# Last down projection and final norm in segments of 384 and 128 tokens instead of 256 and 256

## The chip, the cores and the metric

The kernel runs on one core of a Trainium2 chip. The time is the device time of one execution in microseconds; the time before is the median of 3 runs, 1311.32 us (1310.68 to 1312.76). A core has five engines that run side by side, each with its own instruction list worked off in order: TensorE (PE, matrix products; PEld is its weight load), VectorE (DVE), ScalarE (ACT), GpSimd (POOL) and SyncE (SP, which only issues transfers). They wait for each other through semaphores.

## The reference, cut to what matters

One layer: a half-step SwiGLU FFN on 512 latent and 256 context tokens, a mixer, then for the 512 latent tokens a second half-step FFN and the final RMSNorm. Only the end is touched:

```python
def rmsnorm(x, w):
    xf = x.astype(jnp.float32)
    y = xf * lax.rsqrt(jnp.mean(xf * xf, axis=-1, keepdims=True) + EPS)
    return (y * w.astype(jnp.float32)).astype(x.dtype)

def swiglu(h, w1, w2):
    g, u = jnp.split(h @ w1, 2, axis=-1)
    return (jax.nn.silu(g) * u) @ w2

x = x + 0.5 * gate * swiglu(modulate(rmsnorm(x, norm3_w), shift, scale), w1, w2)   # x: 512 x 1024, w2: 2816 x 1024
return rmsnorm(x, final_norm_w)
```

## The kernel before, in words

Features lie on the partitions and tokens on the free axis: the stream `x` is 8 tiles (m = 0 to 7) of 128 features by 512 tokens, float32. Each float32 product is made as three products of rounded parts (`gemm3`: high by high, high by low, low by high), all of type float32r, which TensorE takes as one instruction, where plain float32 leaves two records in the trace.

The second FFN (`ffn2`) makes 22 hidden tiles of 128 features. Their down projection is done two hidden tiles at a time, 512 tokens wide, while the up projection goes on (`turns`, banks named `aux`). The last two hidden tiles are kept for the end (`last`), and `down_last` does them in two segments of tokens, one after the other; call them A and B. In a segment `down` makes for each m six products (2 hidden tiles by 3) into one bank named `mm` (there are five), then:

- VectorE evicts: `x = bank * gate + x` (`stt`, called the eviction below);
- ScalarE squares x (`sq_add`) into `rms_acc` (the first of a lane) or `nm_t` (the later ones, of which so many buffers are there as `bufs` says), and then scales x in place by the weight of the final norm;
- VectorE (lane v) or GpSimd (lane p) adds `nm_t` to the accumulator of its lane. The last m have lanes of their own, with nothing to add.

When a segment's eight m are out, `after` queues its norm: TensorE sums each accumulator over the partitions by products with a column of ones (`rms_sum`, plain float32, one per accumulator and 128 tokens), VectorE adds the epsilon (`hms`), GpSimd takes the power -1/2 (`hr`), VectorE spreads it over a diagonal (`dg`), TensorE turns this into one row for all partitions (`rms_spread`), VectorE multiplies x by it, two m at a time (`then` in `build`, tile `s`, called the scaling below), and SP sends each pair of m to the output. Behind segment B eight products that nobody reads (`busy` in `after`) run while its norm is waited for.

What sets the order: a scheduler places every engine's instructions when the kernel is built, from the order in which the code calls them and what they depend on. So A's norm is laced into B's products, and the places are fixed before the kernel runs. `sq_add` also serves the end of the first FFN (three segments of 256 tokens) and the end of the mixer, with the same buffer names.

Of the kernel before, what the change touches and what calls it, by code (L numbers as in the profile page):

```python
# [7 lines left out]
F32 = mybir.dt.float32  # L8
# [4 lines left out]
P = 128  # L13
DM = 1024
KT = DM // P
NC_ = 256
# [10 lines left out]
CTX, LAT, LAT_A, LAT_B = (0, NC_), (NC_, NL), (NC_, 256), (NC_ + 256, 256)  # L27
# [42 lines left out]
class Space1:  # L70
# [16 lines left out]
    gate = lambda self, j: self.rows(j, 1)  # L87
# [11 lines left out]
class Builder:  # L99
# [13 lines left out]
    def sq_add(self, S, k, x, n, lanes="vpvpvpvl"):  # L113

        nc = self.nc
        lane = lanes[k]
        if n > 512:
            sq = self.tmp.tile([P, n], F32)
        elif lane in S:
            sq = self.tmp.tile([P, n], F32, name="nm_t", bufs=3)  # L120
        else:
            sq = self.tmp.tile([P, n], F32, name="rms_acc", bufs=6)
        nc.scalar.activation(sq, x, AF.Square)
        if lane not in S:
            S[lane] = sq
            return lambda: None
        eng = nc.gpsimd if lane == "p" else nc.vector
        return lambda: eng.tensor_tensor(out=S[lane], in0=S[lane], in1=sq, op=ALU.add)
# [434 lines left out]
    def ffn2(self, w1, w2, gate, first, then, final, fast):  # L563
        nc = self.nc
        G = 2

        def load2(j):
            w2r = self.fp.tile([P, DM], F32, name="w2raw", bufs=2)
            w2h = self.fp.tile([P, DM], F32R, name="w2hi", bufs=3)
            w2l = self.fp.tile([P, DM], F32R, name="w2lo", bufs=3)  # L570
            nc.sync.dma_start(out=w2r, in_=w2[j])
            return w2h, w2l, w2r

        def mm(part, half, k):
            ws, pss = part
            h, l = (w[:, k * P:(k + 1) * P] for w in ws[half])
            self.gemm3(pss[half], h, l, self.xh[k][:, NC_:], self.xl[k][:, NC_:], k, KT)

        class Space:
            sums = lambda _, j: (fast["s"][:, 2 * (j % 2) + i, :] for i in range(2))  # L580
            last = lambda _: [self.fp.tile([P, DM // 2], F32R, name="wd" + x, bufs=2) for x in "hl"]
            up = lambda _, j: self.fp.tile([P, 2, 256], F32, name="ev", bufs=2)
            gate = lambda _, j: self.fp.tile([P, NL], F32, name="sg", bufs=2)
        space = Space()

        def act_tiles():
            return [self.fp.tile([P, NL], F32R, name=n, bufs=3) for n in ("ah", "al")]

        def gated(part, sg, lo, n):

            g, u = (p[:, lo - NC_:lo - NC_ + n] for p in part[1])
            sg = sg[:, lo - NC_:lo - NC_ + n]
            nc.scalar.activation(sg, g, AF.Silu)
            self.tt(sg, u, sg, ALU.mult)

        def act(part, j):
            w2, sg, (ah, al) = load2(j), space.gate(j), act_tiles()
            gated(part, sg, *LAT)
            self.split(ah, al, sg)
            self.split(*w2)  # L600
            return w2[0], w2[1], ah, al

        def up(j):
            part = self.ffn_load(w1, j)
            for half in range(2):
                for k in range(KT):
                    mm(part, half, k)
            return act(part, j)

        parts, turns, late = [], [], {}  # L610

        def done(part):
            parts.append(part)
            if len(parts) == G:
                both = parts[:]
                parts.clear()
                turns.extend(lambda m=m: self.down(both, LAT, m, 1, self.aux, gate, off=NC_) for m in range(KT))

        def turns_take(n=NT):
            for _ in range(min(n, len(turns))):  # L620
                turns.pop(0)()

        def turn(j, at):
            if at == 3:
                late[j] = load2(j)
                self.split(*late[j])
            if j < NJ - 1 or at in (0, 2, 4):
                turns_take(1)

        def gated_fast(j, sg):  # L630
            ah, al = act_tiles()
            self.split(ah, al, sg)
            done((late[j][0], late[j][1], ah, al))
        for j, part in enumerate(first):
            done(act(part, j))
        for j in range(2, fast["first"]):
            if j == fast["first"] - 1:
                fast["s"] = fast["make"]()
            part = up(j)
            turns_take()  # L640
            done(part)
        unit = lambda j: self.up_half(w1, j, 256, NC_, fast["t"], space, j == NJ - 1)
        nxt = unit(fast["first"])
        next(nxt), next(nxt)
        last = []

        def end(j, sg):

            if j < NJ - 1:
                return gated_fast(j, sg)  # L650
            ah, al = act_tiles()
            for c in (0, 256):
                self.split(*(t[:, c:c + 256] for t in (ah, al, sg)))
            last.extend((*parts, (late[j][0], late[j][1], ah, al)))
        self.ups_half(range(fast["first"], NJ), unit, nxt, turn, end)
        turns_take()
        self.down_last(last, [(seg, gate) for seg in (LAT_A, LAT_B)], then, final=final, off=NC_)

    def fast_operands(self, pool, first=4):

# [914 lines left out]
```

## Time and profile before

| | |
|---|---|
| median of 3 runs | 1311.32 us |
| profiled execution, its own time | 1312.59 us |
| its span in the trace | 1310.8 us |
| PE busy | 1286.0 us (98%) |
| DVE, ACT, POOL busy | 1012.4, 578.0, 56.5 us |
| last product of segment B ends | 1297.56 us |
| last scaling of the norm ends | 1306.78 us |

The span is what the profiler saw from the first to the last instruction; the execution's own time lies 1.79 us above it. PE is busy nearly all the time, so for most of the kernel a change counts only as far as it moves PE. In the last 13 us PE has no more large products, and the time is set by the chain of the norm.

### The profile page before, as it was taken

The page shows a single profiled execution, that of the slowest core. Times are in us where ns is not written, and L with a number is a line of the kernel's source. Part 1 is how long each engine was busy: PE and PEld are TensorE (multiplying, and loading weights), DVE is VectorE, ACT ScalarE, POOL GpSimd, SP SyncE. Part 2 cuts the span into 40 slices and gives each one's busy share as a digit, 9 for nine tenths or more (in the row PEclk, how much of TensorE's full clock was granted, in tenths as well). Part 3 has the DMA queues.
Part 4 walks back from the last instruction along what each step waited for, and adds up shares of the span by engine and source line. Part 5 has one row for each costly group of instructions (what it writes and reads, how often), then busy time and mean ns, then how long its engine had stood idle before and what let it go on. Part 6 is the DMA issues. An engine that isn't in the chain of part 4 may idle for free.

```text
span 1310.8 us, 20560 instructions
## 1 busy us (share of the span) xinstructions
PE 1286.0 (98%) x8210; PEld 1179.8 (90%) x8210; DVE 1012.4 (77%) x1620; ACT 578.0 (44%) x992; POOL 56.5 (4%) x81
## 2 busy tenths in 40 slices
PE   8999999999999999999989999999999999999997
PEld 4689999999998888999978798889998999999996
DVE  6995778777789888767676867986588788888766
ACT  5553444444442222383457343444473444444434
POOL 2000000000000000110100000000000000000001
PEclk8999999999999999999989999999999999999998
DMA  9224443344686866413041101114233222233301
GB/s 347 106 93 151 140 146 125 133 140 145 214 289 228 271 209 195 145 47 117 3 145 49 65 34 49 65 50 175 83 107 136 97 97 97 102 108 104 106 17 65
DMA packets 48803, 163.60 MB, mean 125 GB/s; under 512 B 5554, under 2 KB 10034, under 8 KB 48708
## 3 DMA queue, kind: packets, MB, share of 16 engines
q1 hardware_dynamic: 46308, 150.50, 33.4%
q0 software_dynamic: 2400, 11.80, 2.8%
q8 instruction: 64, 1.05, 0.3%
q14 instruction: 31, 0.25, 0.1%
HBM read 149.39 MB, written 12.89 MB: 124 GB/s over the span
## 4 chain that ended last, share of the span: by engine, by line
PE 94%; DVE 2%; ACT 2%; issue 1%; POOL 0%; DMA 0%; POOLq 0%; DVEq 0%
PE mm L56 72%; PE aux L56 21%; DVE mod_scr L56 1%; ACT xh L56 1%; DVE x L56 0%; ACT nm_y L56 0%; ACT x L56 0%; DVE wlo L56 0%; ACT nm_t L56 0%; ACT whi L56 0%; DVE xl L56 0%; POOL rms_acc L56 0%; DVE s L56 0%; DVE nm_x L56 0%; DMA four<-in_cc 0%
## 5 line engine op out<-in xcount | busy, mean ns | idle before, releaser
L56 PE MATMUL mm<-xh,whi 128*128 128x256 f32 (+2 forms) x1072 | 345.7, 323 | 1.2 <-ACT xh L56 1.2
L56 PE MATMUL mm<-xh,wlo 128*128 128x256 f32 (+2 forms) x1072 | 342.4, 320 | 0.8 <-DVE wlo L56 0.8
L56 PE MATMUL mm<-xl,whi 128*128 128x256 f32 (+2 forms) x1000 | 323.4, 324 | 2.9 <-DVE xl L56 2.9
L56 PEld LDWEIGHTS mm<-xh,whi 128*128 128x128 f32 x1072 | 203.3, 190 | 14.3 <-ACT xh L56 1.9
L56 PEld LDWEIGHTS mm<-xh,wlo 128*128 128x128 f32 x1072 | 203.4, 190 | 10.8 <-DVE wlo L56 1.0
L56 PE MATMUL mm<-six,whi 128*128 128x384 f32 (+1 forms) x752 | 209.3, 359 | 0.0
L56 PEld LDWEIGHTS mm<-xl,whi 128*128 128x128 f32 x1000 | 189.8, 190 | 14.7 <-DVE xl L56 4.3
L56 ACT ACTIVATE whi<-wraw 128x1024 fp32r<-128x1024 f32 x100 | 105.9, 1062 | 170.4 <-PE aux L56 91.5
L56 PEld LDWEIGHTS mm<-six,whi 128*128 128x128 f32 x752 | 135.7, 188 | 10.0
L56 PE MATMUL mm<-six,wlo 128*128 128x384 f32 (+1 forms) x376 | 134.4, 357 | 0.0
L56 DVE TENSOR_TENSOR wlo<-wraw,whi 128x1024 fp32r<-128x1024 f32 x100 | 121.7, 1219 | 10.5 <-ACT whi L56 10.4
L56 DVE CUSTOM_DVE_ANT_0 mod_scr<-wm,cb 128x1024 bf16<-128x1024 f32 x84 | 105.4, 1255 | 2.8 <-DMA wm<-in_w_mod 2.6
L56 PEld LDWEIGHTS mm<-six,wlo 128*128 128x128 f32 x376 | 70.6, 188 | 6.5
L56 DVE SCALAR_TENSOR_TENSOR x<-mm,mod_l,x 128x256 f32<-128x256 f32 (+1 forms) x88 | 51.9, 601 | 18.3 <-PE mm L56 17.5
L56 DVE TENSOR_TENSOR wlo<-four,whi 128x1024 fp32r<-128x1024 f32 x37 | 45.3, 1225 | 26.7 <-ACT whi L56 26.7
L56 PE MATMUL aux<-ah,w2hi 128*128 128x512 f32 x160 | 64.0, 400 | 0.0
L56 ACT ACTIVATE whi<-four 128x1024 fp32r<-128x1024 f32 x37 | 39.2, 1061 | 56.1 <-PE mm L56 46.1
L56 PE MATMUL aux<-al,w2hi 128*128 128x512 f32 x160 | 63.1, 394 | 0.0
L56 DVE SCALAR_TENSOR_TENSOR x<-aux,mod_l,x 128x512 f32<-128x512 f32 x80 | 58.9, 745 | 5.2 <-PE aux L56 5.2
L56 PE MATMUL aux<-ah,w2lo 128*128 128x512 f32 x160 | 62.4, 390 | 0.0
L56 PE MATMUL mm<-tl,whi 128*128 128x256 f32 x216 | 61.0, 283 | 0.0
L56 PE MATMUL aux<-six,whi 128*128 128x256 f32 x320 | 59.0, 282 | 0.0
(336 smaller groups left out, 2553.8 us busy)
## 6 DMA issues: line engine op xcount, KB each, us to landing
wraw<-in_f1w SPq DMA_DIRECT2D x62, 512.0 KB, 3.9
wm<-in_w_mod SPq DMA_DIRECT2D x58, 512.0 KB, 4.0
wraw<-in_f2w SPq DMA_DIRECT2D x44, 512.0 KB, 3.4
wraw<-in_wi SPq DMA_DIRECT2D x32, 512.0 KB, 3.3
w2raw<-in_f2w SPq DMA_DIRECT2D x22, 512.0 KB, 4.2
four<-h SPq DMA_DIRECT2D x22, 384.0 KB, 4.7
h<-x POOLq DMA_DIRECT2D x18, 384.0 KB, 3.0
wraw<-in_wo SPq DMA_DIRECT2D x8, 512.0 KB, 4.0
```

Source lines behind the costliest of these rows:

```text
L56: r = f(*a, **kw)
```

## The change

Segments A and B of `down_last` in `ffn2` are 384 and 128 tokens instead of 256 and 256. To fit in memory, `nm_t` has 2 buffers instead of 3 and `rms_acc` 3 instead of 6, everywhere that `sq_add` is called; squares of 128 tokens get a name of their own with 4 buffers.

```diff
         elif lane in S:
-            sq = self.tmp.tile([P, n], F32, name="nm_t", bufs=3)
+            sq = self.tmp.tile([P, n], F32, name="nm_t", bufs=2)
+        elif n == P:
+            sq = self.tmp.tile([P, n], F32, name="rms_last", bufs=4)
         else:
-            sq = self.tmp.tile([P, n], F32, name="rms_acc", bufs=6)
+            sq = self.tmp.tile([P, n], F32, name="rms_acc", bufs=3)
...
-        self.down_last(last, [(seg, gate) for seg in (LAT_A, LAT_B)], then, final=final, off=NC_)
+        self.down_last(last, [((NC_, 384), gate), ((NC_ + 384, P), gate)], then, final=final, off=NC_)
```

The order moves in two places. First VectorE at the end, from the first scaling of segment A on (`s` is the scaled output, `x<-mm` an eviction of B, `hms` the start of B's norm). Before:

```order
L56 TENSOR_TENSOR s<-x,aux 128x2x256
L56 SCALAR_TENSOR_TENSOR x<-mm,mod_l,x 128x256
L56 TENSOR_TENSOR rms_acc<-rms_acc,nm_t 128x256
L56 TENSOR_TENSOR s<-x,aux 128x2x256
L56 SCALAR_TENSOR_TENSOR x<-mm,mod_l,x 128x256
L56 TENSOR_TENSOR s<-x,aux 128x2x256 x2
L56 TENSOR_SCALAR hms<-aux 128x2
```

The same stretch now, with the last three evictions of B between the scalings:

```order
L56 TENSOR_TENSOR s<-x,aux 128x2x384
L56 TENSOR_TENSOR rms_last<-rms_last,nm_t 128x128
L56 TENSOR_TENSOR s<-x,aux 128x2x384
L56 SCALAR_TENSOR_TENSOR x<-mm,mod_l,x 128x128
L56 TENSOR_TENSOR s<-x,aux 128x2x384
L56 SCALAR_TENSOR_TENSOR x<-mm,mod_l,x 128x128
L56 TENSOR_TENSOR s<-x,aux 128x2x384
L56 SCALAR_TENSOR_TENSOR x<-mm,mod_l,x 128x128
L56 TENSOR_SCALAR hms<-aux 128x1
```

Before, two scalings stood ahead of the last eviction and two behind it; now all four, each half as wide again, stand ahead of it, and three evictions stand behind the first scaling instead of two.

The second place is TensorE at the start of the mixer's projections, where the norm of the first FFN's last segment is summed (`rms_acc` 5029, 5047, 5128 are its three accumulators). Here the sums stand in the difference as taken out:

```order
 L56 MATMUL mm_5138<-xh_86,whi_4801 128x256
-L56 MATMUL aux_5201<-ones_80,rms_acc_5029 128x1 x2
-L56 MATMUL aux_5201<-ones_80,rms_acc_5047 128x1 x2
-L56 MATMUL aux_5201<-ones_80,rms_acc_5128 128x1 x2
 L56 MATMUL mm_5138<-xl_87,whi_4801 128x256
```

And here as put in, six products later:

```order
 L56 MATMUL mm_5138<-xh_86,whi_4801 128x256
+L56 MATMUL aux_5201<-ones_80,rms_acc_5029 128x1 x2
+L56 MATMUL aux_5201<-ones_80,rms_acc_5047 128x1 x2
+L56 MATMUL aux_5201<-ones_80,rms_acc_5128 128x1 x2
 L56 MATMUL mm_5138<-xl_87,whi_4801 128x256
```

The sums of that segment moved behind six products of 256 columns.

## Rows read from the trace of the kernel before

**Rows 1.** The page's chain that ended last: shares of the span by engine.
```profile
PE 94%; DVE 2%; ACT 2%; issue 1%; POOL 0%; DMA 0%; POOLq 0%; DVEq 0%
```
**Rows 2.** Stretches: us, busy by engine (instructions), granted clock (1.00 is full), DMA, GB/s.
```profile
1283.45:1297.56 14.11, 13.96 (x111) 13.34 (x109) 11.74 (x27) 10.89 (x30) 3.47 (x5) 1.00 0.01 2
1297.56:1306.78 9.22, 4.40 (x26) 3.62 (x26) 5.91 (x12) 2.14 (x5) 1.08 (x2) 0.67 0.41 145
1306.78:1310.80 4.02, 0.00 (x0) 0.00 (x0) 0.00 (x0) 0.00 (x0) 0.00 (x0) 0.50 0.55 189
```
**Rows 3.** Timeline of PE at the end: start, us, instruction, count [idle before it].
```profile
1292.33 1.05 PE L56 MATMUL aux<-ones,rms_acc 128*128 128x1 f32 x8
...
1297.28 0.28 PE L56 MATMUL mm<-ah,w2lo 128*128 128x256 f32 x1
1298.27 0.61 PE L56 MATMUL aux<-ones,rms_acc 128*128 128x1 f32 x4 [0.71 <-DVE rms_acc L56]
...
1300.66 0.82 PE L56 MATMUL aux<-ones,rms_acc 128*128 128x1 f32 x4
1303.07 1.19 PE L56 MATMUL aux<-dg,ones 128*128 128x256 f32 x2 [1.59 <-DVE dg L56]
```
**Rows 4.** Timeline of DVE at the end.
```profile
1286.46 2.05 DVE L56 SCALAR_TENSOR_TENSOR x<-mm,mod_l,x 128x256 f32<-128x256 f32 x5 [0.26 <-PE mm L56]
...
1297.53 0.68 DVE L56 TENSOR_TENSOR rms_acc<-rms_acc,nm_t 128x256 f32<-128x256 f32 x1
...
1298.74 0.47 DVE L56 SCALAR_TENSOR_TENSOR x<-mm,mod_l,x 128x256 f32<-128x256 f32 x1
...
1302.49 0.42 DVE L56 TENSOR_TENSOR dg<-ident,hr 128x256 f32<-128x256 f32 x1 [0.82 <-POOL hr L56]
1304.30 2.48 DVE L56 TENSOR_TENSOR s<-x,aux 128x512 f32<-128x512 f32 x4 [1.38 <-PE aux L56]
```
**Rows 5.** Timeline of ACT at the end.
```profile
1290.67 0.71 ACT L56 ACTIVATE nm_t<-x 128x256 f32<-128x256 f32 x2
...
1292.09 0.71 ACT L56 ACTIVATE rms_acc<-x 128x256 f32<-128x256 f32 x2
...
1299.24 0.42 ACT L56 ACTIVATE rms_acc<-x 128x256 f32<-128x256 f32 x1 [0.38 <-DVE x L56]
```
**Rows 6.** Chain, merged: products of 384 columns, then of 256 (start, us, count).
```profile
299.90 30.16 PE mm L56 x174
...
1248.02 2.87 PE mm L56 x24
```
**Rows 7.** Timeline of PE in the mixer: plain float32 products of 128 columns.
```profile
714.76 1.05 PE L56 MATMUL aux<-d,w 128*128 128x128 f32 x8
```
**Rows 8.** Groups of instructions by form: count, busy us, mean ns, idle before.
```profile
L56 DVE SCALAR_TENSOR_TENSOR d<-d,t3a,aux 128x128 f32<-128x128 f32 x32 | 9.3, 344 | 6.6 <-PE aux L56 4.3 <-ACT d L56 2.2
...
L56 ACT ACTIVATE w<-w 128x128 f32<-128x128 f32 x16 | 4.8, 298 | 8.8 <-DVE w L56 8.8
...
L56 ACT ACTIVATE w<-w 128x256 f32<-128x256 f32 x2 | 0.8, 418 | 1.4 <-DVE w L56 1.4
...
L56 POOL TENSOR_TENSOR hr<-hms,mhalf 128x2 f32<-128x2 f32 x8 | 6.4, 805 | 74.5 <-DVE hms L56 74.5
L56 POOL TENSOR_TENSOR hr<-hms,mhalf 128x4 f32<-128x4 f32 x5 | 5.2, 1033 | 133.0 <-DVE hms L56 133.0
```
**Rows 9.** Transfers: queue, count, KB each, median us from issue to landing.
```profile
out<-s SPq DMA_DIRECT2D x8, 256.0 KB, 2.3
...
wm<-in_pen SPq DMA_DIRECT2D x1, 128.0 KB, 2.0
```
**Rows 10.** Timeline of PE, then of ACT, at the start of the mixer's projections.
```profile
566.97 1.40 PE L56 MATMUL aux<-ones,rms_acc 128*128 128x1 f32 x12
...
573.91 0.39 PE L56 MATMUL mm<-xl,whi 128*128 128x256 f32 x1 [0.30 <-DVE xl L56]
...
571.05 0.60 ACT L56 ACTIVATE xh<-nm_x,mod_l 128x256 fp32r<-128x256 f32 x1 [1.33 <-DVE nm_x L56]
```

## The prediction

> **What bounds the kernel now.** I read the chain that ended last first [rows 1]: 94% of it is PE, so nearly everywhere the kernel is as long as its products. Then the end, cut into three stretches [rows 2]. From 1283.45 to 1297.56 PE does segments A and B (96 products) and A's norm, and is busy 13.96 of 14.11 us. From 1297.56 to 1306.78 only the norm of B runs: PE is busy 4.40 of 9.22 us and no engine is full; that is a chain, and each link of it counts. From 1306.78 to 1310.80 only the last transfer and the end of the program are left, 4.02 us. The timelines show who is late in the first two stretches: the last product starts at 1297.28, but the last eviction only at 1298.74 [rows 3, 4], because scalings of A stand ahead of it on DVE, and the sums of B run from 1298.27 to 1301.48 on PE [rows 3].
>
> A wider A makes the part under PE longer, a narrower B makes the chain behind it shorter. The two have to be set against each other.
>
> **Products of A.** 174 products of 384 columns took 30.16 us, 0.173 each; 24 of 256 took 2.87, 0.120 each [rows 6]. A has 48: 8.3 us instead of 5.7, so A's products end at 1283.45 + 8.3 = 1291.8.
>
> **Products of B.** Their number stays 48 and each is half as wide. No float32r product under 256 columns is in the trace, so I bound it. The line through 0.173 and 0.120 gives some 0.065 at 128 columns. Sums of one column follow each other at (1.05 - 0.25)/7 = 0.114 [rows 3], 0.25 being the one that ends last: loading 128 columns of weights takes this long whatever follows. Plain float32 products of 128 columns leave two records 0.11 apart [rows 7], 0.22 for a product. I take 0.114, since B's products load as much weight as these; so B costs 5.5 us, hardly less than 48 x 0.120 = 5.7. The Trainium skill has a rule against this change here ("TensorE: Matmul & The Clock Gate", section "LDWEIGHTS (loading the stationary operand)"): the load takes time by its columns of weights, 128 over 1.2 GHz, and not by what streams through. By that B would be at least an estimated 5.1 us, by the line above 3.1; the rows of one column are on the rule's side.
>
> **Norm of A.** ACT does a square and a scaling for each m: two m in 1292.09 - 1290.67 = 1.42 us [rows 5], 0.71 for one. An ACT instruction grows by 0.12 us from 128 to 256 columns [rows 8]; at 384 a pair takes 0.71 + 0.22, about 0.93. A's first eviction starts near 1286.6 instead of 1286.46 [rows 4] and takes 0.6, so the eighth square is done near 1287.2 + 7 x 0.93 + 0.5 = 1294.2. PE reaches the sums after two m of B, at 1291.8 + 12 x 0.114 = 1293.1, and waits for the last added square until about 1293.6. They are 18 records now instead of 12: 2.05 us, to 1295.7. Then the step on DVE and the power with 3 columns: hr grows by 0.11 a column from 2 to 4 [rows 8], so 0.82, and dg 0.55: ready at 1297.4. PE does three m of B first (18 x 0.114 = 2.05, to 1297.8) and then the spread of 384 columns, some 0.95: 1298.7.
>
> **The scalings of A, now ahead of the last eviction.** An eviction of 256 columns follows the next at 0.41 (2.05 over 5), one of 128 columns has 344 ns against 470 [rows 4, 8]: 0.13 per 128 columns. Four scalings of 512 took 2.48 us [rows 4], 0.62 each; at 768 0.62 + 0.27 = 0.89. By the new order DVE does four of these (3.55), three evictions (0.28 each, 0.84) and one add (0.2) from 1298.7 on: 4.6 us, to 1303.3. PE has made B's last product by 1300.8, so DVE is what is late next. Before, the last eviction ended at 1298.74 + 0.47 = 1299.21 [rows 4]: this point comes 4.1 us later.
>
> **The chain behind it.** Before, 1299.21 to 1306.78: 7.57 us. Now, hops included: square 0.33 (0.42 less 0.12 [rows 5, 8]); the last sum 0.44, two records at the slow pace of 0.19 ((0.82 - 0.25)/3 [rows 3]) with nothing left ahead of them, since the other sums and the eight idle products fit into the waits of DVE; DVE 0.19; hr 0.69 (0.805 for two columns less 0.11 [rows 8]); dg 0.32 [rows 4]; the spread of 128 columns 0.85 (1.19 halved, with its start [rows 3]); four scalings of 256 columns, 0.35 each, 1.5. That is 4.3 us: 3.3 won back. The last scaling ends at 1307.6. An add on DVE took 0.68 instead of the usual 0.43 where GpSimd added beside it [rows 4]; I put 0.25 on top for that, 1307.9: 1.1 us later than before. The last transfer is 128 KB instead of 256: 2.0 against 2.3 us [rows 9], 0.3 back. The end costs 0.8 us.
>
> **Fewer buffers.** At the end of the first FFN the sums of the last segment move behind six products, 0.72 us. They stood at 566.97 [rows 10], DVE waits for them in order and is ahead of ACT, and PE later waits for what ACT makes: the idle 0.30 at 573.91 [rows 10] ends with that chain. PE has done the six products earlier by then, so it waits 0.7 more. The bounds: nothing, if ACT's wait of 1.33 at 571.05 [rows 10] has other reasons, and 1.4 if ACT's squares also wait for buffers. I take 0.7. Elsewhere the squares wait for adds that DVE has done before the next eviction anyway: nothing; if that cover went, 0.4 (an add) per m of A, at most 2 us on the path by 1294.2.
>
> **The sum.** +0.8 and +0.7 is +1.5. The profiled execution took 1312.59, so it would take 1314.1; it lies 1.27 above the median of the runs shown. For the median I predict 1311.32 + 1.5 = 1312.8 us. By itself, with 0.065 to 0.12 for B's product and 0 to 1.4 for the buffers, this runs from 1311.7 to 1314.2.
>
> **Rival 1, narrow products take two passes.** At 0.22 each B takes 10.7 us; its last product ends near 1305.5, 2.2 behind DVE's 1303.3, with eviction and start 2.8 later. Then 1315.6. For: plain float32 at this width does it, and no float32r product of the kernel is under 256 columns. Against: a float32r product of 256 or more columns is one record at one pace.
>
> **Rival 2, the clock falls earlier.** The granted clock is 1.00 up to the last product and 0.67 in the stretch behind it [rows 2], after PE had waited 0.71 [rows 3] and then done only sums and small products; the levels are 2.4 and 1.2 GHz. Now PE waits 0.5 at 1293.1, sums, and streams half as many columns per product. Should it fall there, B's 18 products before the spread cost (0.19 - 0.114) x 18 = 1.4 more and the spread 0.95: 2.3 later on DVE too. Then 1315.1. Against: before, the clock held through 12 sums and two waits in the first stretch. The Trainium skill ("TensorE: Matmul & The Clock Gate", section "What's actually happening") has the gate follow how busy PE has recently been; weight loads stay near full here, and no row tells whether these count.
>
> **Rival 3, faster.** If the four scalings of A do not hold up the last eviction, the chain starts from PE's last product: 1300.8 + 0.6 + 4.3 = 1305.7, 1.1 before the old 1306.78, with the transfer 1.4; 1309.9 with the buffers free. With 0.065 per product it is some 2 us less, 1308. It decides at 0.3 us per scaling instead of 0.89, or at a spread before 1296.4. For: DVE idles between evictions while A is worked off. Against: the order of DVE is fixed, and the scalings cannot begin before the spread.
>
> **How the numbers follow.** The forecast has 0.58, rival 1 0.18, rival 2 0.12, rival 3 0.12. No change means within 0.2%, 1308.7 to 1313.9, which is about what a measurement here can tell. Slower holds rivals 1 and 2 nearly whole (0.29) and an eighth of the forecast (0.07): 0.36. Faster holds a third of rival 3 and a little of the rest: 0.05. The same: 0.59. The range reaches below into rival 3 and above past rivals 1 and 2: 1310.4 to 1316.2; some 0.08 is left out on each side.
>
> **What would show it.** In the profile after: A's products at 0.173 and B's at about 0.114; a wait of PE of about 0.5 us ahead of the 18 sums; the last eviction ending near 1303.3, on DVE straight behind a scaling, with PE done over 2 us before; about 4.3 us from there to the last scaling. At the start of the mixer's projections ACT's wait ends 0.7 later. Wrong would be: a last product later than the scalings (rival 1 or 2; pace and clock part them), or a last eviction that waits for PE's last product (rival 3).

## The result and the profile after

The changed kernel takes 1319.17 us (median of 6 runs, 1317.43 to 1321.60), the kernel before beside it 1311.83. The ratio is 1.0051 with a 95% interval of 1.0041 to 1.0061: 5.4 to 8.0 us slower. I had forecast 1.5 us more, with a range up to 1316.2; the range does not hold the time. The clock of TensorE fell in the middle of segment B, which the prediction had as rival 2, with a chance of 0.12 and a price of 2.3 us; both were too small.

The profiled execution of the changed kernel took 1321.6 us, the longest of its six, and 9.0 more than that of before. Here are its stretches from A's first product to the end (us, busy by engine with instructions, granted clock, DMA share, GB/s): A's products, then B up to the end of the last eviction, then the chain behind it, then the last transfer.

```profile
1285.58:1294.23 8.65, 8.65 (x51) 8.48 (x50) 7.33 (x13) 5.48 (x13) 1.02 (x1) 1.00 0.01 3
1294.23:1310.05 15.82, 14.83 (x73) 14.08 (x73) 8.98 (x19) 7.79 (x21) 2.77 (x4) 0.59 0.16 59
1310.05:1316.07 6.02, 3.25 (x14) 2.90 (x14) 1.87 (x7) 0.71 (x2) 0.56 (x1) 0.50 0.30 108
1316.07:1319.78 3.71, 0.00 (x0) 0.00 (x0) 0.00 (x0) 0.00 (x0) 0.00 (x0) 0.50 0.48 137
```

Before, A and B ran at 1.00 to the last product [rows 2]. Now the second stretch has a mean clock of 0.59; cut where the clock changes, it is two:

```profile
1294.23:1296.92 2.69, 1.70 (x16) 1.55 (x15) 2.44 (x5) 2.69 (x7) 1.00 (x1) 1.00 0.00 0
1296.92:1310.05 13.13, 13.13 (x59) 12.52 (x59) 6.53 (x15) 5.09 (x15) 1.77 (x3) 0.50 0.20 72
```

The timeline of PE shows what stands there, first the start of B, then its rest:

```profile
1294.13 0.27 PE L56 MATMUL mm<-al,w2hi 128*128 128x128 f32 x1
1294.24 0.27 PE L56 MATMUL mm<-ah,w2lo 128*128 128x128 f32 x1
...
1296.51 3.65 PE L56 MATMUL aux<-ones,rms_acc 128*128 128x1 f32 x18 [0.99 <-DVE rms_acc L56]
1300.03 0.45 PE L56 MATMUL mm<-ah,w2hi 128*128 128x128 f32 x1
1300.28 0.41 PE L56 MATMUL mm<-al,w2hi 128*128 128x128 f32 x1
1300.49 0.41 PE L56 MATMUL mm<-ah,w2lo 128*128 128x128 f32 x1
...
1303.90 1.59 PE L56 MATMUL aux<-nm_x,ones 128*128 128x384 f32 x2
...
1310.48 1.84 PE L56 MATMUL aux<-xh 128*128 128x256 f32 x7
1312.12 0.42 PE L56 MATMUL aux<-ones,rms_last 128*128 128x1 f32 x2
1313.85 0.77 PE L56 MATMUL aux<-dg,ones 128*128 128x128 f32 x2 [1.31 <-DVE dg L56]
```

B's products start 0.11 apart (1294.13, 1294.24). Behind the wait of 0.99, 0.41 us into the 18 sums, the clock falls to 0.5 (1296.92): the sums take 3.65 us, and the products behind them start 0.213 apart. The chain that ended last runs straight over them:

```profile
1296.51 3.65 PE aux L56 x18
1300.16 3.94 PE mm L56 x18
1304.11 1.40 PE aux L56 x2
```

On DVE, the scalings of A and the last eviction come behind that:

```profile
1305.53 0.95 DVE L56 TENSOR_TENSOR s<-x,aux 128x768 f32<-128x768 f32 x1 [1.03 <-PE aux L56]
...
1308.85 0.94 DVE L56 TENSOR_TENSOR s<-x,aux 128x768 f32<-128x768 f32 x1
1309.71 0.34 DVE L56 SCALAR_TENSOR_TENSOR x<-mm,mod_l,x 128x128 f32<-128x128 f32 x1
1312.57 0.16 DVE L56 TENSOR_SCALAR hms<-aux 128x1 f32<-128x1 f32 x1 [2.52 <-PE aux L56]
...
1314.65 1.42 DVE L56 TENSOR_TENSOR s<-x,aux 128x256 f32<-128x256 f32 x4 [0.95 <-PE aux L56]
```

The last eviction stands directly behind a scaling, as forecast, but ends at 1310.05. Against [rows 4], counted from A's first product (1285.58 here, 1283.45 before), it ends 24.5 us in instead of 15.8, the last scaling 30.5 instead of 23.3, the span 34.2 instead of 27.3. So 6.9 of the 9.0 us lie in the end. The other 2.1 lie before it: 0.1 from the start of the program, 1.26 between 540 and 600 us, where the buffers are fewer, and 0.7 in the mixer. The buffers' place on ACT, where the first FFN's last segment is squared:

```profile
565.50 0.42 ACT L56 ACTIVATE nm_t<-x 128x256 f32<-128x256 f32 x1 [0.30 <-POOL rms_acc L56]
...
566.77 0.42 ACT L56 ACTIVATE nm_t<-x 128x256 f32<-128x256 f32 x1 [0.54 <-POOL rms_acc L56]
```

Before, one square there waited for GpSimd:

```profile
564.79 0.42 ACT L56 ACTIVATE nm_t<-x 128x256 f32<-128x256 f32 x1 [0.24 <-POOL rms_acc L56]
```

With two buffers the squares wait 0.84 us for GpSimd's adds instead of 0.24, the sums stand six products later, and everything behind moves.

### The profile page after: what moved, and what is told of

It reads as the page before. It is cut to its first block, busy times and chain, and to the rows that moved or that the text cites. A ratio compares the mean times of both kernels' runs of the same rounds, so it can differ in the third digit from the quotient of the medians.

```text
span 1319.8 us, 20553 instructions
## 1 busy us (share of the span) xinstructions
PE 1295.4 (98%) x8208; PEld 1188.5 (90%) x8208; DVE 1012.2 (77%) x1620; ACT 578.4 (44%) x992; POOL 56.3 (4%) x81
## 4 chain that ended last, share of the span: by engine, by line
PE 93%; DVE 2%; ACT 2%; issue 1%; DMA 0%; POOL 0%; SPq 0%; POOLq 0%; DVEq 0%; ACTq 0%
PE mm L56 71%; PE aux L56 21%; DVE mod_scr L56 1%; DMA x<-in_xT 0%; ACT xh L56 0%; ACT six L56 0%; ACT nm_y L56 0%; ACT x L56 0%; DVE wlo L56 0%; ACT nm_t L56 0%; DVE x L56 0%; DVE s L56 0%; ACT whi L56 0%; DVE xl L56 0%; ACT rms_acc L56 0%
## 5 line engine op out<-in xcount | busy, mean ns | idle before, releaser
L56 DVE SCALAR_TENSOR_TENSOR x<-mm,mod_l,x 128x512 f32<-128x512 f32 (+3 forms) x88 | 51.9, 600 | 18.4 <-PE mm L56 17.6
```

What stands on the lines that cost most here:

```text
L56: r = f(*a, **kw)
```

## The experiments

Each ran beside the kernel before on the same chip; times are medians. "Above before" is worked out from the measured ratio of the two times, with its 95% interval in brackets. "From A's first product" is counted inside one profile. Runs without an interval are single executions. A profile shows one execution of a kernel's several, and not always a typical one.

**The changed kernel again.**

> The changed kernel once more, for a second profile: its first profiled execution was the longest of its runs. If the fall of the clock belongs to the order of the work, it comes at the same place to within a us or two (behind B's first 12 products); if it is chance, it comes elsewhere, and the time moves with it. The stretch at half clock at 730 us is there again if it belongs to the order of the work.

1318.97 us. The clock fell at 1298.84, 13.8 us from A's first product instead of 11.3, and the last scaling ended at 28.3 instead of 30.5. So the fall belongs to the order of the work, its moment shifts by a few us, and the end of the kernel moves with it: 32.05 us from A's first product instead of 34.2. The stretch at half clock at 730 us was there again. Of the kernels below it shows in three, one of them with all the buffers, and not in the others, so I take it for chance. It goes with a shorter stretch at 660 us (3.4 us instead of 6.8); together they cost 0.5 us against before (products lie 1.39 us further back at 640 us, 1.86 at 760).

**Only the buffers.** `nm_t` 3 to 2 and `rms_acc` 6 to 3 in the kernel before.

> The kernel before with its segments of 256 and 256 tokens, and only the buffers taken away (nm_t 2, rms_acc 3). In the changed kernel the products of the first FFN's end and the start of the mixer lie 1.25 us later than before (0.14 us behind at 548, 1.39 behind at 570). Theory A: the buffers do this, and the end with two equal segments loses little, so the time is 0.7 to 1.8 us above before. Theory B: the buffers are hidden, and the shift belongs to something else: within 0.4 us of before. The changed kernel also had a stretch of 3.4 us at granted clock 0.5 at 730 us in the mixer, which before had not; if the shift of the work brings it, it is seen here too, otherwise it is chance.

1313.01 against 1312.53: 0.5 us above before (-0.7 to 1.7). The profile has the shift in its place: products lie 1.23 us further back at 600 than at 540 us. In all ten profiles with fewer buffers this shift was 1.2 to 1.3 us. In this execution the end was 1.1 us shorter than in the profile of before (26.25 against 27.32 from A's first product); the clock fell 2.5 us later there (19.8 us from A's first product instead of 17.2). Theory A holds for the place; the whole is within what two medians can part.

**B over 256 columns.**

```diff
+        pad = 256 - w if S is not None and w < 256 else 0
...
-                self.gemm3(banks[m - m0][:, :w], h[:, ms], l[:, ms], ah[:, lo - off:lo - off + w],
-                           al[:, lo - off:lo - off + w], q, len(parts))
+                at = lo - off
+                self.gemm3(banks[m - m0][:, :w + pad], h[:, ms], l[:, ms], ah[:, at - pad:at + w],
+                           al[:, at - pad:at + w], q, len(parts))
...
-            self.stt(x, banks[m - m0][:, :w], gate[:, m:m + 1], x, ALU.mult, ALU.add)
+            self.stt(x, banks[m - m0][:, pad:pad + w], gate[:, m:m + 1], x, ALU.mult, ALU.add)
```

> The changed kernel, but each product of segment B runs over 256 columns instead of 128 (the 128 extra columns are tokens of A computed a second time and read by nobody), at about 0.120 us instead of 0.111. PE still waits for A's last square before the sums. Theory S (the clock follows what PE streams: narrow products and one-column sums let it fall at 1297): the clock stays at 1.00 through A's sums and to about the end of B, the spread and the last eviction come some 4 us earlier, and the time is 1314 to 1316. Theory W (the wait of 1 us ahead of the 18 sums lets it fall): the clock falls at about 1297 all the same, and the time is 1318 to 1321.

1315.91: 3.4 us above before (2.0 to 5.0), within theory S. But in the profiled execution, the longest of its six (1319.13), the clock was not held. From A's last product to the last eviction, cut where it changed:

```profile
1295.78:1299.77 3.99, 3.59 (x31) 3.39 (x31) 2.51 (x5) 3.77 (x10) 1.01 (x1) 1.00 0.00 0
1299.77:1306.60 6.83, 6.83 (x31) 6.22 (x30) 2.82 (x7) 2.10 (x7) 1.46 (x2) 0.50 0.00 0
1306.60:1308.74 2.14, 2.14 (x20) 2.14 (x20) 2.03 (x7) 1.32 (x4) 0.46 (x1) 1.00 0.48 182
```

The sums stand in two groups here, twelve records from 1298.08 and six from 1300.60. The clock fell between them and came back among the wide products. Neither theory says that. Of the other executions only the mean clock of the whole program is known: 0.991 to 0.992 in the three shortest (1314.22 to 1314.93), 0.987 to 0.988 in the three longest; the changed kernel's six have 0.985 to 0.988. Wide products alone may have held the clock in the shorter ones; no profile shows it, and the mean takes in the start of the program, where executions differ too (ahead of 50 us, 17.1 us at half clock in this profile and 10.2 in that of before; at 100 us its products lie 1.93 us further back).

The scheduler also placed VectorE's work otherwise. Here, and in every kernel below with B widened to 256 columns, two scalings of A stand behind the last eviction; in the changed kernel none does. So what these kernels win is not the clock's alone.

**No wait ahead of A's sums.**

```diff
-        self.todo += [None, lambda: (sums(), diag()), None, None, spread, *more]
+        late = n == 384
+        self.todo += [None, *[None] * (2 * late), lambda: (sums(), diag()), None, None, spread, *more]
```

> The changed kernel, with A's 18 sums two m of B later, behind 24 narrow products instead of 12, so that PE does not wait ahead of them; the spread keeps its distance of three m behind the sums. Theory W (the wait lets the clock fall): no wait, the clock stays at 1.00 through the sums at about 1297 to 1299, and the time is 1314 to 1316. Theory S (narrow products and one-column sums let it fall): the clock still falls between 1296 and 1299, and the time is 1318 to 1321.

1316.90: 4.3 above (2.6 to 6.0). In its profile, the longest of five, PE had no idle time from A's last product on, and the clock fell:

```profile
1295.51:1299.71 4.20, 4.20 (x40) 4.20 (x40) 2.77 (x6) 4.17 (x12) 1.01 (x1) 1.00 0.00 0
1299.71:1307.77 8.06, 8.06 (x36) 7.45 (x35) 4.68 (x12) 3.52 (x11) 1.74 (x3) 0.50 0.02 7
```

So the wait is not needed for the fall. Theory W is out. The time lies between the two forecasts: most of the sums were over by then and took 2.34 us, not 3.65; and here, too, two scalings of A stand behind the last eviction.

**Narrow products, and one-column sums, by themselves.** Three kernels put work that nobody reads ahead of segment A of the kernel before.

```diff
+            for _ in range(108):
+                self.nc.tensor.matmul(bank[:, :P], lhsT=self.xh[0][:, :P], rhs=self.xh[0][:, :P], start=True, stop=True)
```

The second kernel has instead of these:

```diff
+            for _ in range(54):
+                self.nc.tensor.matmul(bank[:, :1], lhsT=self.ones, rhs=self.ones[:, :1], start=True, stop=True)
```

> The kernel before with 108 products of float32r over 128 columns, which nobody reads, ahead of segment A (1283 us), behind products of 512 columns and with no wait and no one-column sum among them. Theory S1 (narrow products alone let the clock fall): the granted clock is 1.00 for the first 3 to 6 us of them and 0.5 behind that, the pace goes from 0.111 to 0.213, and they take 15 to 20 us. Theory S2 (they hold the clock; what lets it fall are the one-column sums or the wait): clock 1.00, 0.111 each, 12.0 us in all, and the rest as before.

> The kernel before with 54 plain float32 products of one column (108 records), which nobody reads, ahead of segment A, with no wait among them. Theory: one-column sums let the clock fall, 3 to 6 us behind the last product of 512 columns, the pace goes from 0.114 to 0.2 a record, and they take 15 to 20 us. Rival (PE counts as busy while it loads weights): clock 1.00, 0.114 a record, 12.3 us.

The narrow products, one row of the timeline: 12.17 us, 0.111 apart, and the clock stayed at 1.00 (1324.01 us).

```profile
1284.07 12.17 PE L56 MATMUL aux<-xh 128*128 128x128 f32 x108
```

The one-column sums, cut where the clock changed (1333.19 us):

```profile
1283.65:1286.74 3.09, 3.09 (x30) 3.09 (x28) 2.55 (x4) 0.96 (x3) 0.00 (x0) 1.00 0.02 5
1286.74:1303.86 17.12, 17.12 (x82) 17.12 (x81) 0.00 (x0) 0.00 (x0) 0.00 (x0) 0.50 0.00 0
```

So S1 is out: narrow products alone hold the clock. Sums alone lose it, though both PE and its weight load are recorded as busy all the time. The sums are plain float32 and the products float32r, so the two runs differ in type as well as in columns, and no run parts these. The Trainium skill ("TensorE: Matmul & The Clock Gate", section "What's actually happening") has the gate follow how busy PE has been; the prediction left open whether weight loads count, and here a PE that only loads weights and streams one column lost the clock.

Then sums first, and narrow products behind them:

> The kernel before with 27 plain float32 products of one column (54 records) and behind them 108 float32r products of 128 columns ahead of segment A, none of them read, no wait among them. The sums let the clock fall, 3 us in. Theory H (narrow products hold a full clock but do not bring a fallen one back): all 108 run at 0.213, 23 us, and the clock rises only under segment A; about 1343 us. Theory R (they bring it back as wider ones do): it rises 3 to 7 us into them, the rest runs at 0.111, 13 to 17 us; 1333 to 1337 us.

```profile
1289.62:1312.90 23.28, 23.28 (x110) 23.28 (x111) 0.00 (x0) 0.00 (x0) 0.00 (x0) 0.50 0.00 1
```

All 108 ran at half clock, 0.213 apart (1342.77 us); it rose only under segment A's products of 256 columns, 3.0 us into them. Theory H holds in this run: narrow products keep what they find. It fits that the changed kernel does not recover in either profile, while the kernel with 256 columns in B did. The Trainium skill ("TensorE: Matmul & The Clock Gate", section "LDWEIGHTS (loading the stationary operand)") gives the load by its columns over 1.2 GHz, without the clock; 0.111 agrees, 0.213 at half clock does not.

**B over 256 columns, and wide products around A's sums.** Four products of 512 columns in the wait, one behind each of the first two accumulators.

> The changed kernel with B's products over 256 columns (half of them computed a second time and read by nobody) and six products of 512 columns that nobody reads around A's sums: four in the wait ahead of them (0.9 us), one behind the sums of each of the first two accumulators. If the fall of the clock is what separates the change from its forecast of +1.5 us, the clock now stays at 1.00 to the end of B, the rest of the end goes as forecast and the time is 1.0 to 2.5 us above before. If the end costs more for other reasons (scalings on VectorE, the chain behind the last eviction), it stays 3 us or more above before.

1315.58: 3.0 above (1.7 to 4.2), outside the first theory's 1.0 to 2.5 and at the edge of the second. The clock still fell, for 3.4 us (1298.56 to 1301.97), and PE had 1.4 us more to do. Not conclusive.

**A's sums apart.** One accumulator after each of B's second, third and fourth m.

```diff
+            accs = [S[q] for q in "pvl"]
+            one = lambda at: self.rms_sum(accs, n, box, at)
+            self.todo += [None, lambda: one(0), lambda: one(1), lambda: (box.update(ms=one(2)), diag()), spread, *more]
```

> The changed kernel, with A's 18 one-column sums cut into three groups of 6, one accumulator after each of B's second, third and fourth m, six narrow products between the groups; the spread stands where it stood. Theory (an unbroken stretch of one-column sums and waiting lets the clock fall, narrow products hold it): the clock stays at 1.00 at least to the end of B (about 1302), the last eviction comes 3 to 4 us earlier than in the changed kernel, and the time is 1.0 to 2.5 us above before. Rival (18 sums are too many however they lie): it falls near 1297 to 1299 as in the changed kernel, and the time is 5 to 7 us above before.

1319.27: 6.0 above (4.5 to 7.7). A miss: six narrow products between six sums do not hold the clock, even in the shortest of its five executions, which is the profiled one (1317.58).

```profile
1292.16:1297.16 5.00, 4.42 (x41) 4.27 (x40) 3.35 (x8) 4.85 (x13) 1.00 (x2) 1.00 0.00 0
1297.16:1306.02 8.86, 8.21 (x35) 7.41 (x35) 5.91 (x12) 2.84 (x8) 1.75 (x3) 0.50 0.29 106
```

**Both: B over 256 columns and A's sums apart.**

> The changed kernel with both: B's products over 256 columns (half of them read by nobody) and A's 18 sums in three groups with six products between. Nothing is added to PE's work but the columns (48 times 0.009, 0.4 us). Theory (A's sums, the wait and narrow products together let the clock fall; either alone does not cure it): the clock stays at 1.00 to the end of B, the last eviction comes 4 to 5 us earlier than in the changed kernel, and the time is 0.8 to 2.2 us above before, as forecast. Rival (terms off the clock were mis-sized too): the clock holds and the time is still 3 us or more above before.

In the profiled execution the clock is held to the end of B:

```profile
1285.57:1294.21 8.64, 8.64 (x51) 8.46 (x50) 7.33 (x13) 5.45 (x13) 1.00 (x1) 1.00 0.01 3
1294.21:1305.49 11.28, 10.19 (x79) 9.25 (x78) 7.46 (x18) 7.22 (x21) 2.77 (x5) 1.00 0.08 29
1305.49:1310.61 5.12, 1.61 (x11) 1.26 (x9) 3.50 (x9) 0.71 (x2) 0.56 (x1) 0.66 0.67 246
```

The end takes 28.77 us from A's first product, 1.45 more than before (27.32) and 5.4 less than in the changed kernel's first profile, 3.3 less than in its second. The time is 1315.96: 3.7 above before (2.1 to 5.2), more than the 0.8 to 2.2 that I expected. In its profiled execution (1316.16) the rest lies ahead of A's first product: 2.1 us, of which 1.2 at the buffers. By the time, then, wide products alone (3.4 above) did as much as both edits. The end of VectorE's work on A shows the other order:

```profile
1305.15 0.35 DVE L56 SCALAR_TENSOR_TENSOR x<-mm,mod_l,x 128x128 f32<-128x128 f32 x1
1305.41 1.81 DVE L56 TENSOR_TENSOR s<-x,aux 128x768 f32<-128x768 f32 x2
1307.13 0.16 DVE L56 TENSOR_SCALAR hms<-aux 128x1 f32<-128x1 f32 x1
```

**Without the eight idle products.** `then(seg, box), 8 if end else 0)` becomes `then(seg, box), 0)`; in the changed kernel, in the last one, and twice in the kernel before.

> The changed kernel without the eight products of 256 columns that nobody reads behind segment B. In the changed kernel seven of them stand at half clock between the sums of the last accumulator but one and the last, 1.84 us from 1310.48. Theory: they are on the path, and the chain behind the last eviction (6.0 us) falls to 4.3 to 4.9 us, the time by 1 to 1.7 us against the changed kernel (about 1317.5). Rival (the wait for the last square covers them, as predicted): within 0.4 us of the changed kernel.

1317.03: 4.5 above before (2.8 to 6.2), 2 us under the changed kernel (in another session). The last sums follow one another, and from the last eviction to the last scaling it is 4.52 us instead of 6.02:

```profile
1308.66 2.02 PE L56 MATMUL aux<-ones,rms_last 128*128 128x1 f32 x8
```

> The same without the eight products that nobody reads behind B. At full clock they took 0.3 to 0.5 us between the last sums where B's products had 256 columns. Theory: the chain behind the last eviction is 4.3 to 4.6 us and the time 0.2 to 0.6 us below the kernel with them, so 0.4 to 1.8 us above before. Rival: without them the clock falls under the last sums and the time is the same or up to 1 us more.

1315.64, 4.1 above (2.6 to 5.6), more than the 0.4 to 1.8 that I expected, and 4.82 us for the chain, also more: with the clock held the idle products were worth 0.3 us of the chain. The clock did not fall earlier without them.

> The kernel before without the eight products of 256 columns that nobody reads behind segment B. There B's sums and these products follow each other on PE without a gap from 1298.50 to 1302. Theory: they are on the path, and the time falls by 0.5 to 1.5 us. Rival: without them the clock falls earlier or the sums wait for the last square anyway, within 0.4 us of before.

> The kernel before without the eight products that nobody reads, once more, beside the version with both edits: its interval reached from 2.2 us below before to 0.1 above. If they are on the path it is 0.7 to 1.3 us below before again; if the first result was chance, within 0.4 us.

1311.57 against 1312.88, 1.1 below before (2.2 below to 0.1 above), and again 1311.42 against 1312.49, 1.3 below (2.5 to 0.1 below). In the profile the 16 records of B's sums take 2.10 us in a row and end 1.1 us earlier from A's first product:

```profile
1299.37 2.10 PE L56 MATMUL aux<-ones,rms_acc 128*128 128x1 f32 x16 [0.72 <-DVE rms_acc L56]
```

By its median this kernel is the fastest of all, though 0.1% is little, and one of the two intervals reaches past zero.

**One scaling of A moved behind the last eviction**, in the kernel before, alone and with the idle products out.

```diff
-                self.tick()
+                if not end or len(self.todo) > 3:
+                    self.tick()
...
+            rest, self.todo = (self.todo, []) if end else ([], self.todo)
             self.after(seg, S, lambda box, seg=seg: then(seg, box), 8 if end else 0)
+            self.todo[2:2] = rest
```

(`rest` is what is left of A's scalings; it now comes behind B's sums in the list.)

> The kernel before (256 and 256 tokens, all buffers) with one scaling of A less ahead of the last eviction: it moves behind it, where VectorE waits for B's sums anyway. If scalings ahead of the last eviction put off the chain behind it, the last eviction comes 0.7 us earlier and the time is 0.4 to 0.8 us below before (1.0 at most). If the chain waits for something else (the sums' place on PE, the adds), the time is within 0.3 us of before.

> The kernel before (256 and 256 tokens, all buffers) with two edits at its end: the eight products that nobody reads behind B left out, and one scaling of A moved behind the last eviction. Each alone: without the products the last sums ended 1.1 us earlier after A's start and the time was 1.0 us lower (interval from 2.2 lower to 0.1 higher); the moved scaling put the last eviction 0.6 us earlier and the time did not change, because the idle products held PE. Theory: together the earlier eviction reaches the sums, 1.3 to 1.8 us below before. Rival: the sums wait for a square or an add all the same, and it is as without the products alone, 0.5 to 1.1 us below.

Alone it changed nothing: 1312.78 against 1312.17 (-1.2 to 1.2), though the last eviction came 0.6 us earlier from A's first product; PE's sums and idle products filled the time. With both, 1311.42 against 1312.49, 0.7 below (1.8 below to 0.5 above), the same as without the idle products alone. B's sums start when VectorE's last add is done, 0.71 us of waiting, whatever happens to the eviction behind it. So in the kernel before, the last eviction was not the link that I took it for.

## Why the prediction was wrong

**Right, by its steps.** A's products end 8.65 us from their start, 2.55 later than before (forecast 2.6). B's narrow products take one pass, 0.111 each at full clock (0.114); rival 1 is out. The order on DVE does what was said: all scalings of A stand ahead of the last eviction, 0.95 and 0.94 each (0.89). The last transfer is 0.3 shorter (0.3).

**The step that failed is the clock.** The forecast took 1.00 to the end of B, and rival 2 was held against with "before, the clock held through 12 sums and two waits". There the sums stood among products of 256 columns. In the changed kernel the clock fell inside B in both profiles. In the first, the 18 sums, the 18 products behind them and the spread took 3.65, 3.94 and 1.40 us, 9.0 us on the chain for a forecast of 5.05.

What lets it fall is shown in part. By themselves, narrow products keep a clock, sums lose it, and narrow products do not bring it back, one execution each. The wait ahead of the sums is not needed. The six more records of sums (18 instead of 12) are not it in the first profile, where the clock fell 0.41 us into them. That the width of B matters fits the times: the four kernels with B widened to 256 columns lie 3.0 to 4.1 us above before, those with 128 columns 4.3 to 6.7. Whether it takes sums laced among the wide products as well is not shown.

**And its price.** Rival 2 had 2.3 us: 1.4 for the 18 products ahead of the spread and 0.95 for the spread. From A's first product, the forecast had the last eviction end 19.85 us in and the last scaling 24.45; the two profiles of the changed kernel have 24.5 and 22.3, and 30.5 and 28.3. I had left out that the sums themselves run at half clock (3.65 us for a forecast of 2.05), and that the clock stays low for all that follows, the idle products too.

Between the medians of the changed kernel and the one with the clock held it is 3.2 us (1319.17 and 1315.96, in two sessions), but that holds VectorE's other order too: two scalings, 1.81 us, stand behind the last eviction. The kernel without the wait has this order as well, lost the clock and lies 4.3 above before. How the 3.2 us divide between clock and order is open. With the clock held the last eviction ends 19.9 us in, as forecast, but that is luck: the first scaling starts at 17.1, where the forecast had 15.25, and two scalings fewer stand ahead of it.

**Smaller steps.** Fewer buffers cost 1.25 us at their place, not 0.7; the forecast had 1.4 as the end of its range, "if ACT's squares also wait for buffers", and they do, for GpSimd's adds. PE's wait ahead of the 18 sums was 0.99, not 0.5, since A's squares and adds ran later. "The eight idle products fit into the waits of DVE" was wrong: seven of them stand on the path, 1.84 us at half clock. The chain is 6.0 us instead of 4.3; without them 4.5, and 4.8 where the clock was held and two scalings of A stood in its way. With the clock held the last scaling ends 1.7 us later than before; the forecast was 1.1, and the wider columns of that kernel can be 0.4 of the difference (an estimate: 48 products at 0.120 instead of 0.111).

**The sum now.** 1.25 us for the buffers and 1.45 for the end with the clock held give 2.7. That kernel lies 3.7 above before; its interval (2.1 to 5.2) takes 2.7 in, and in its profile 0.9 lies ahead of A's first product and not at the buffers. With the 3.2 from there to the changed kernel the sum is 5.9, of the 5.4 to 8.0 that were measured.

## What to carry to other kernels

A narrower segment at the end is not a shorter end if its products are limited by loading weights: 128 columns cost 0.111 us and 256 cost 0.120. And the clock can go with it: 12 sums of one column ran at full clock among products of 256 columns in the kernel before; among those of 128 columns the clock fell and did not come back. Wide products are no guarantee: in one profile it fell among them too, and came back after 6.8 us. When work is thinned out on the engine that bounds the kernel, price the whole rest of the program at the lower clock. And ask of every filler instruction whether it stands on the path there.

## What was not expected of the hardware

- 108 products of float32r over 128 columns kept the granted clock at 1.00 for 12.17 us, but at 0.50 for 23.28 us when they found it there.
- PE and its weight load were recorded as busy for all of 17.12 us of one-column sums, at a granted clock of 0.50.
- At half clock products of 128 columns start 0.213 us apart, and so do one-column records; at full clock both start 0.111 apart. What bounds them slows with the clock.
- The fall came at different moments in two executions of one kernel (11.3 and 13.8 us from A's first product), and the end was 2.15 us shorter in the second. The runs of the changed kernel spread over 4.2 us; those of the kernel before over 2.1 in the six beside it, and over 4.7 in twenty of a later session (1310.40 to 1315.06).
